# A two-layer decoder trunk on one core: where the second layer's wide Gram copies, Gram products and masks stand in the order of the work

## The chip, the core and the metric

The kernel runs on one core of a Trainium2 chip. Time is what the device needs for one execution, in microseconds (us); the median of the runs counts, and less is better. The engines are named as in the profile: PE (TensorE, matmuls), PEld (PE's weight loads, which overlap its matmuls), DVE (VectorE), ACT (ScalarE), POOL (GpSimd) and SP (SyncE, which here only starts transfers). Each engine carries out its own instructions strictly in the order in which they were put into its queue.

## The reference

Two residual layers over 512 positions of width 2048. Layer 0 is gated differential attention, which the change does not touch. Layer 1 is gated RWKV-7 time mixing with 32 heads of width 64:

```python
def step(S, inp):
    r_t, w_t, k_t, v_t, a_t, b_t = inp
    sa = jnp.einsum('bhvk,bhk->bhv', S, a_t)
    S = S * w_t[:, :, None, :] + sa[..., None] * b_t[:, :, None, :] + v_t[..., None] * k_t[:, :, None, :]
    y = jnp.einsum('bhvk,bhk->bhv', S, r_t)
    return S, y
...
p = h @ w_in                                  # 2048 -> 4*2048 + 2*96
p = p + (token_shift(p) - p) * mu
r, k, v, g, dw, da = jnp.split(p, RW_SPLITS, axis=-1)
...
y = wkv7_scan(rh, heads(decay), kh, vh, -kk, kk * ah)
y = (y - mean) * lax.rsqrt(var + GN_EPS)      # per head, then gain, bias and a bonus term
y = y.reshape(B, T, RW_WIDTH) * jax.nn.silu(g)
return y @ w_out, v_first                     # and x + this
```

All in float32, so each large product is computed as three matmuls on operands that are split into a high and a low part.

## The kernel before, in words

**Split products.** A weight tile `wraw` (eight blocks of 128x128) is loaded by SP, cast by ACT to its high part `wh` (L115), and DVE subtracts to get the low part `wl` (L116), four blocks at a time. One projection of 128 columns is 16 blocks of three matmuls with 512 columns (L129): 48 on PE. `unit_chan` issues them, and after every block a *hook* may run: `behind=[(18, f)]` calls `f` when 18 of the 48 have been issued.

**Rounds.** Layer 1 runs 16 rounds, j = 0 to 15, each for one pair of heads: the projections to keys (`proj(1, j)`), receptances (`proj(0, j)`), values (`proj(2, j)`) and, three rounds later, gates (`proj(3, j - 3)`). The scan of pair j − 1 runs inside round j.

**The chunked scan.** 512 positions are eight chunks of 64. For every pair three things are made first. `gram` (L1136): 32 small matmuls into four PSUM tiles `gp` (tags pb and pc, two buffers each), from which ACT copies the small triangles `LP` (eight copies of 32x128, L1144) and the wide Gram matrices `G` (four copies of 128x512, L1148); in the kernel before the two kinds alternate on ACT as the scheduler chooses. `mask_gram`: four affine selects on POOL (L1174, L1176) that zero parts of `G`. `t_solve`: a triangular solve on DVE, which begins with the transpose `LT` of `LP` (L1208) and goes on in pairs of small steps (L1221, L1224), paced by PE's matmuls, until the transposes to `T` (L1229) and `W` (L1234); then `t_first` (px products, L1255) and `t_second` (L1270) make the inverse `TT` with POOL's and ACT's help.

`scan_pair` then does, for each chunk c, on one PSUM tile `sm`:

- W: one product of G and VS (L1347); ACT copies the result to `rhs` (L1350, two copies)
- X: one product of TT and `rhs` (L1360); ACT copies it into `VS` (L1362, two copies)
- K: one product of BKT and VS (L1367); DVE adds the decayed state and writes the next chunk's `VS` (L1374 for c = 0, L1371 after)

The next W needs that VS. So the scan is a chain PE, ACT, PE, ACT, PE, DVE, and the kernel fills the time between its products with the matmuls of the projections: a `Chain` object counts matmuls (`tick`) and issues the next product after a fixed number, the gaps: (7, 8) in rounds 3 to 14, (5, 6) in round 2, (4, 5) in rounds 1 and 15.

**What sets the order.** A scheduler orders each engine's queue by readiness and priority: scan (`SCAN`) before solve (`SOLVE`) before work marked `AHEAD` (weight splits, the LP copies, the group norm) before the rest, where the G copies are. `issue_after` ties a piece of work behind an instruction in the order. `g.soon` is a list of deferred pieces; `soon(g)` issues all that is in it, and `scan_pair` calls it right behind the copies of `rhs`, inside a scan step:

```python
for h, r_ in HEADS:
    rc = nc.scalar.copy(rhs[r_, :], sm[r_, h * C : h * C + C])
with g.tc.issue_after(rc.ins):
    soon(g)
```

**Neighbours.** `norms` sends sums of squares (`ssl`, L1160) through DRAM with POOL's transfers `nd<-ssl` and `n<-nd` (L1164, L1167); the buffer of `ssl` is shared with `ysq` (L1414), the squares of the group norm of pair j − 2, which is followed on DVE by a sum, a Newton rsqrt (L63 to L70) and a product with `yc` (L1420). `turn_keys` transposes the keys (L1189) to `BKT` (L1190).

Of the kernel before, what the change touches and what calls it, by code (L numbers as in the profile page):

```python
# [23 lines left out]
P = 128  # L24
D = 2048
# [886 lines left out]
def split_act(g, src, pool, tag):  # L912
    nc = g.nc
    hh = pool.tile(list(src.shape), F32R, name="sH" + tag, tag=tag + "H", bufs=1)
    hl = pool.tile(list(src.shape), F32R, name="sL" + tag, tag=tag + "L", bufs=1)
    nc.scalar.copy(hh[:], src)
    nc.vector.tensor_sub(hl[:], src, hh[:].bitcast(F32))
    return hh, hl


def unit_chan(g, parts, cols, step=P, more=None, behind=(), pts=None):

    nc = g.nc
    n = cols // step
    pts = pts or [g.pp.tile([P, 512], F32, name="pp", tag="pp") for _ in range(n)]
    KG = 8 if cols == P else 4
    m = None
    for k0 in range(0, KT, KG):
        wh, wl = split_w(g, parts, KG, cols, k0)
        for k, c in [(k, c) for k in range(KG) for c in range(n)]:  # L930
            s = slice(c * step, (c + 1) * step)
            kk = k0 + k
            if more and c == 0:
                more(kk + 2, m)
            m = mm3(nc, pts[c][:step, :], wh[:, k, s], wl[:, k, s], g.hH[kk][:], g.hL[kk][:],
                    kk == 0, kk == KT - 1, g)
            for at, follow in behind:
                if 3 * kk + 3 == at:
                    follow(m)
    return pts  # L940


@urgent
def shift_mix(g, ps, rows, mu, omu, tag, bufs=2):

    nc, w = g.nc, g.work
    o_ = w.tile([P, T], F32, name="mix" + tag, tag=tag, bufs=bufs)
    nc.scalar.activation(o_[:rows, :], ps[:rows, :], AF.Copy, scale=omu)
    nc.vector.scalar_tensor_tensor(o_[:rows, 1:], ps[:rows, 0 : T - 1], mu, o_[:rows, 1:], ALU.mult, ALU.add)
    return o_  # L950
# [84 lines left out]
def mus(g, i, j):  # L1035
    n = i * 16 + j
    return g.mu[:, n : n + 1], g.omu[:, n : n + 1]


def sum_channels(g, out, ones, x):  # L1040

    h, l = x
    g.nc.tensor.matmul(out, ones, h[:], start=True, stop=False)
    g.nc.tensor.matmul(out, ones, l[:], start=False, stop=True)


def soon(g):
    while g.soon:
        g.soon.pop(0)()
# [76 lines left out]
def gram(g, j, p):  # L1126

    nc, w, BK = g.nc, g.work, p.BK
    p.G = w.tile([P, NC_, 2, 2, C], F32, name="G1", tag="G1", bufs=2)
    halves = []  # L1130
    for c0, tag in ((0, "pb"), (4, "pc")):
        gp = [g.ps.tile([P, 512], F32, name="gp", tag=tag, bufs=2) for _ in range(2)]
        halves.append((c0, gp))
        for i in range(4):
            for h, r_ in ((0, slice(0, C)), (1, slice(C, P))):
                m = nc.tensor.matmul(gp[h][:, i * P : (i + 1) * P], BK[r_, c0 + i, :, :], p.AR[r_, c0 + i, :, :],  # L1136
                                     start=True, stop=True)
    p.LP = w.tile([P, NC_, HALF], F32, name="LP", tag="tmpl", bufs=1)
    with g.tc.high_priority(offset=AHEAD):
        for c0, gp in halves:  # L1140
            for h in range(2):
                for half in range(2):
                    q, o = h * C + half * HALF, half * HALF
                    nc.scalar.copy(p.LP[q : q + HALF, c0 : c0 + 4],  # L1144
                                   gp[h][q : q + HALF].rearrange("p (u x) -> p u x", u=4)[:, :, o : o + HALF])
    for c0, gp in halves:
        for h in range(2):
            nc.scalar.copy(p.G[:, c0 : c0 + 4, :, h, :], gp[h][:].rearrange("p (u x t) -> p u x t", u=4, x=2))  # L1148


def norms(g, j, p, m):
# [18 lines left out]
def mask_gram(g, p, h, m=None):  # L1170

    nc = g.nc
    for r_ in [slice(h * C, h * C + C)]:
        a = nc.gpsimd.affine_select(out=p.G[r_, :, 0, 1 - h, :], in_=p.G[r_, :, 0, 1 - h, :], compare_op=ALU.is_ge,  # L1174
                                fill=0.0, base=-1, pattern=[[0, NC_], [1, C]], channel_multiplier=-1)
        b = nc.gpsimd.affine_select(out=p.G[r_, :, 1], in_=p.G[r_, :, 1], compare_op=ALU.is_ge, fill=0.0, base=0,  # L1176
                                pattern=[[0, NC_], [0, 2], [1, C]], channel_multiplier=-1)
        behind(g, a, m)
        behind(g, b, m)


def turn_keys(g, p, c0):

    nc = g.nc
    if not c0:
        p.BKT = g.work.tile([P, NC_, P], F32, name="BKT", tag="BKT", bufs=2)
    ps = g.ps.tile([P, 512], F32, name="pt", tag="pb", bufs=2)
    for i in range(4):
        nc.tensor.transpose(ps[:, i * P : (i + 1) * P], p.BK[:, c0 + i].rearrange("p s t -> p (s t)"), g.ident[:])  # L1189
    nc.scalar.copy(p.BKT[:, c0 : c0 + 4], ps[:].rearrange("p (c k) -> p c k", c=4))  # L1190


def behind(g, ins, m=None):

    m = m or g.at
    if m:
        g.tc.add_manual_dep(ins.ins, m.ins.name, mybir.DependencyInfo(mybir.DependencyClass.NoSync,
                            mybir.DependencyReason.DATA), reason="pace")
# [80 lines left out]
def stage_v(g, j, p, vps):  # L1279
    nc, w = g.nc, g.work  # L1280
    col = lambda n: g.prm[n][:, j : j + 1]
    ps = g.ps.tile([P, 512], F32, name="pt", tag="pd", bufs=1)
    sum_channels(g, ps[:], g.ones[:], split_act(g, p.rf[:], w, "x"))
    v = shift_mix(g, vps, P, *mus(g, 2, j), "v", 1)
    p.y = w.tile([P, T], F32, name="y", tag="y", bufs=4)
    nc.vector.tensor_mul(p.y[:], ps[:], v[:])
    nc.scalar.activation(p.y[:], p.y[:], AF.Identity, bias=col("hgb"))
    p.v = v


def turn_values(g, p):

    nc, w, v = g.nc, g.work, p.v
    p.VS = w.tile([P, NC_, 2, C], F32, name="VS", tag="VS", bufs=2)
    ps = g.ps.tile([P, 512], F32, name="pt", tag="pd", bufs=1)
    for t in range(NT):
        nc.tensor.transpose(ps[:, t * P : (t + 1) * P], v[:, t * P : (t + 1) * P], g.ident[:])
    pv = ps[:].rearrange("p (t h n) -> p t h n", t=NT, h=2)
    for h in range(2):
        for par in range(2):  # L1300
            nc.scalar.copy(p.VS[(1 - h) * C : (2 - h) * C, par : NC_ : 2, h, :], pv[par * C : par * C + C, :, h, :])
# [130 lines left out]
def layer1(g, aps):  # L1432
    nc, tc = g.nc, g.tc
    with ExitStack() as cx:
# [7 lines left out]
        def proj(i, j, **k):  # L1442
            return unit_chan(g, [(win, i * D + j * P, P)], P, **k)[0]
# [24 lines left out]
        for j in range(D // P):  # L1468
            p = pairs[j]
            if j:  # L1470
                others = [(1, lambda p=p: turn_keys(g, p, 0)), (2, lambda p=p: turn_keys(g, p, 4)),
                          (4, lambda p=p: turn_values(g, p))]
                if j > 1:
                    others.append((5, lambda i=j - 2: finish_y(g, i, pairs[i])))
                full = LAG <= j < D // P - 1
                gaps = (7, 8) if full else (5, 6) if j == 2 else (4, 5)
                chain(g, j - 1, pairs[j - 1], 3 if j > 1 else 22, *gaps, others)
            stage2(g, j, r, p)

            def behind(m, j=j, p=p):  # L1480
                if j > 1:
                    pairs[j - 2].chain.finish(g)
                with tc.issue_after(m.ins):
                    gram(g, j, p)
                if j + 1 == D // P:
                    mask_gram(g, p, 0)
                    mask_gram(g, p, 1)
                p.solve = Solve(g, t_solve(g, j, p))
            stage_v(g, j, p, proj(2, j, behind=[(18, behind)]))
            if j == 0:  # L1490
                turn_keys(g, p, 0)
                turn_keys(g, p, 4)
                turn_values(g, p)
            if j + 1 < D // P:
                begin(j + 1)
            if j >= LAG:
                gated(g, j - LAG, pairs[j - LAG], gate(g, j - LAG, proj(3, j - LAG)))
            if j + 1 < D // P:
                r = receptances(j + 1)
                if j:  # L1500
                    with tc.high_priority(offset=AHEAD):
                        group_norm(g, j - 1, pairs[j - 1])
# [53 lines left out]
        for nm in ("11", "21", "22", "12"):  # L1556
            t, c = PLACES[nm]
# [66 lines left out]
```

## Time and profile before

| | |
|---|---|
| median of 3 runs | 2167.13 us (2166.67 to 2170.02) |
| the profiled execution | 2167.93 us, its span 2166.2 us |
| mean granted clock of PE | 0.998 |
| PE, PEld busy | 98%, 81% of the span |
| DVE, ACT, POOL busy | 71%, 52%, 15% |

The profile is of one execution, 0.80 us above the median. A row of its timeline has the start (us from the span's start), the duration, the engine, the line, the operation with what it writes and reads, the shape, and, in brackets, how long the engine had been idle and who released it. Layer 1's rounds lie between 1030 and 1990 us. A matmul's rows and its weight load's (PEld) are apart; of the load it is read when PE first could not go on.

### The profile page before, as it was taken

The page shows a single profiled execution, that of the slowest core. Times are in us where ns is not written, and L with a number is a line of the kernel's source. Part 1 is how long each engine was busy: PE and PEld are TensorE (multiplying, and loading weights), DVE is VectorE, ACT ScalarE, POOL GpSimd, SP SyncE. Part 2 cuts the span into 40 slices and gives each one's busy share as a digit, 9 for nine tenths or more (in the row PEclk, how much of TensorE's full clock was granted, in tenths as well). Part 3 has the DMA queues.
Part 4 walks back from the last instruction along what each step waited for, and adds up shares of the span by engine and source line. Part 5 has one row for each costly group of instructions (what it writes and reads, how often), then busy time and mean ns, then how long its engine had stood idle before and what let it go on. Part 6 is the DMA issues. An engine that isn't in the chain of part 4 may idle for free.

```text
span 2166.2 us, 34954 instructions
## 1 busy us (share of the span) xinstructions
PE 2132.2 (98%) x12260; PEld 1755.7 (81%) x12260; DVE 1544.3 (71%) x4137; ACT 1124.0 (52%) x2587; POOL 334.1 (15%) x614
## 2 busy tenths in 40 slices
PE   9999999999999999999999999999999999999999
PEld 8888888888888878888777888888888888877887
DVE  5665647465656667467788888888888888887645
ACT  6443444343444455345566656666666666665333
POOL 0000000000000000021132322323333332232001
PEclk9999999999999999999999999999999999999999
DMA  6223232222223365662222232322223223345565
GB/s 196 90 87 98 79 102 85 96 95 86 92 88 98 98 204 189 181 139 80 81 59 55 76 81 79 82 76 76 76 76 86 76 66 81 84 123 185 178 168 121
DMA packets 258624, 225.77 MB, mean 104 GB/s; under 512 B 12336, under 2 KB 220480, under 8 KB 258448
## 3 DMA queue, kind: packets, MB, share of 16 engines
q1 hardware_dynamic: 239504, 188.03, 29.2%
q0 software_dynamic: 10080, 19.50, 4.5%
q10 hardware_dynamic: 8864, 16.01, 2.0%
q8 instruction: 96, 1.57, 0.3%
q14 instruction: 80, 0.66, 0.1%
HBM read 207.50 MB, written 15.99 MB: 103 GB/s over the span
## 4 chain that ended last, share of the span: by engine, by line
PE 89%; DVE 5%; ACT 4%; issue 1%; DMA 1%; POOL 0%; DVEq 0%; ACTq 0%; POOLq 0%
PE pp L129 69%; PE pt L129 5%; ACT G L1148 1%; ACT LP L1144 1%; PE o L129 1%; PE sc L129 1%; PE sm L1360 1%; PE sm L1367 1%; PE sm L1347 1%; PE lora L129 1%; DVE wl L116 1%; PE gp L1136 1%; PE Y L1389 1%; DMA yr<-yd 1%; PE pt L346 1%
## 5 line engine op out<-in xcount | busy, mean ns | idle before, releaser
L116 DVE TENSOR_TENSOR wl<-wraw,wh 128x512 fp32r<-128x512 f32 (+1 forms) x636 | 446.8, 705 | 388.3 <-ACT wh L115 379.3
L115 ACT CAST wh<-wraw 128x512 fp32r<-128x512 f32 (+1 forms) x636 | 393.1, 619 | 524.4 <-PE pp L129 416.9
L129 PE MATMUL pp<-wh,hH 128*128 128x512 f32 x1268 | 500.1, 394 | 0.8 <-DVE prmin_rw_mu_dram L234 0.6
L129 PE MATMUL pp<-wh,hL 128*128 128x512 f32 x1268 | 497.5, 393 | 0.0
L129 PE MATMUL pp<-wl,hH 128*128 128x512 f32 x1268 | 497.0, 392 | 0.0
L129 PE MATMUL pp<-hH,wh 128*128 128x512 f32 x1024 | 418.3, 408 | 0.0
L129 PE MATMUL pp<-hL,wh 128*128 128x512 f32 x1024 | 414.0, 404 | 0.0
L129 PE MATMUL pp<-hH,wl 128*128 128x512 f32 x1024 | 413.9, 404 | 0.0
L129 PEld LDWEIGHTS pp<-wh,hH 128*128 128x128 f32 x1268 | 238.3, 188 | 49.1 <-issue 1.3
L129 PEld LDWEIGHTS pp<-wh,hL 128*128 128x128 f32 x1268 | 238.2, 188 | 48.6
L129 PEld LDWEIGHTS pp<-wl,hH 128*128 128x128 f32 x1268 | 238.3, 188 | 46.8
L129 PEld LDWEIGHTS pp<-hH,wh 128*128 128x128 f32 x1024 | 193.5, 189 | 38.3 <-issue 2.0
L129 PEld LDWEIGHTS pp<-hH,wl 128*128 128x128 f32 x1024 | 193.9, 189 | 33.4
L129 PEld LDWEIGHTS pp<-hL,wh 128*128 128x128 f32 x1024 | 193.8, 189 | 32.3
L1355 POOL COPY SA<-VS 64x64 f32<-64x64 f32 x224 | 78.6, 351 | 470.5 <-DVE VS L1371 411.2
L1221 DVE SCALAR_TENSOR_TENSOR tmpl<-LT,n,Tm 128x60 f32<-128x60 f32 (+24 forms) x496 | 136.3, 275 | 13.8
L500 POOL DMA_DIRECT2D frow<-yd x12 | 8.9, 742 | 803.1 <-DVE rs_t L67 675.7
L1224 DVE TENSOR_TENSOR Tm<-Tm,tmpl 128x60 f32<-128x60 f32 (+24 forms) x496 | 112.0, 226 | 13.0
L1362 ACT COPY VS<-sm 64x64 f32<-64x64 f32 x256 | 52.9, 207 | 61.3 <-PE sm L1360 49.4
L1350 ACT COPY rhs<-sm 64x64 f32<-64x64 f32 x256 | 52.8, 206 | 58.4 <-PE sm L1347 56.3
L1360 PEld LDWEIGHTS sm<-rhs,TT 128*128 128x128 f32 x256 | 46.1, 188 | 29.9 <-ACT rhs L1350 18.4
L1371 DVE SCALAR_TENSOR_TENSOR VS<-sm,gam,Sg 64x64 f32<-64x64 f32 x192 | 54.1, 282 | 20.0 <-PE sm L1367 15.4
(339 smaller groups left out, 3263.9 us busy)
## 6 DMA issues: line engine op xcount, KB each, us to landing
wraw<-in_rw_w_in_dram SPq DMA_DIRECT2D x128, 512.0 KB, 4.0
wraw<-in_da_w_in_dram SPq DMA_DIRECT2D x254, 256.0 KB, 3.0
wraw<-in_da_w_out_dram SPq DMA_DIRECT2D x26, 512.0 KB, 4.3
wraw<-in_rw_w_out_dram SPq DMA_DIRECT2D x26, 512.0 KB, 4.2
yr<-yd SPq DMA_DIRECT2D x28, 256.0 KB, 3.5
frow<-yd POOLq DMA_DIRECT2D x12, 512.0 KB, 6.1
xq<-in_x_dram SPq DMA_DIRECT2D x16, 256.0 KB, 5.4
xd<-xq ACTq DMA_DIRECT2D x16, 256.0 KB, 3.9
```

What stands on the lines that cost most here:

```text
L115: nc.scalar.copy(hi[:], raw[:, k : k + n])
L116: nc.vector.tensor_sub(lo[:], raw[:, k : k + n], hi[:].bitcast(F32))
L129: m = nc.tensor.matmul(out, a, b, start=s, stop=e, skip_group_check=skip)
L346: nc.tensor.transpose(pt[:, c * P : (c + 1) * P], t1s[t][:, c * P : (c + 1) * P], g.ident[:])
L1136: m = nc.tensor.matmul(gp[h][:, i * P : (i + 1) * P], BK[r_, c0 + i, :, :], p.AR[r_, c0 + i, :, :], start=True, stop=True)
L1221: st = nc.vector.scalar_tensor_tensor(tt, LT[:, i : i + 1, i + 1 :].to_broadcast([P, s, n]), n2[:, i : i + 1], Tm[:, 0:s, i : i + 1].to_br ...
L1224: nc.vector.tensor_add(Tm[:, 0:s, i + 1 :], Tm[:, 0:s, i + 1 :], tt)
L1350: rc = nc.scalar.copy(rhs[r_, :], sm[r_, h * C : h * C + C])
L1355: nc.gpsimd.tensor_copy(p.SA[r_, c - 1, :], VS[r_, c, h, :])
L1360: nc.tensor.matmul(sm[:, P : P + C], both(g.TT[j % 2][:, c]), rhs[:], start=True, stop=True)
L1362: nc.scalar.copy(VS[r_, c, h, :], sm[r_, P : P + C])
L1371: g.state = nc.vector.scalar_tensor_tensor(VS[r_, c + 1, h, :], s_, p.gam[r_, c : c + 1], Sg[r_, :], ALU.mult, ALU.add)
```

## The change

Three edits, all in layer 1.

1. In `gram` the four wide G copies become a function `grams` that is put on `g.soon`, so that they are issued right behind the next copies of `rhs`, as part of the scan step. In round 0, where no scan runs, they are issued at once.
2. The hook that calls `gram` stands at 12 matmuls of the values' projection instead of 18 in rounds 1 and 2.
3. In round 15 the masks (`mask_gram`) are issued at 39 matmuls of that projection instead of together with `gram`.

```diff
-    for c0, gp in halves:
-        for h in range(2):
-            nc.scalar.copy(p.G[:, c0 : c0 + 4, :, h, :], gp[h][:].rearrange("p (u x t) -> p u x t", u=4, x=2))
+
+    def grams():
+        for c0, gp in halves:
+            for h in range(2):
+                nc.scalar.copy(p.G[:, c0 : c0 + 4, :, h, :], gp[h][:].rearrange("p (u x t) -> p u x t", u=4, x=2))
+
+    g.soon.append(grams)
+    if not j:
+        soon(g)
...
                 with tc.issue_after(m.ins):
                     gram(g, j, p)
-                if j + 1 == D // P:
-                    mask_gram(g, p, 0)
-                    mask_gram(g, p, 1)
                 p.solve = Solve(g, t_solve(g, j, p))
-            stage_v(g, j, p, proj(2, j, behind=[(18, behind)]))
+            hooks = [(12 if 0 < j < 3 else 18, behind)]
+            if j + 1 == D // P:
+                hooks.append((39, lambda m, p=p: [mask_gram(g, p, h, m) for h in range(2)]))
+            stage_v(g, j, p, proj(2, j, behind=hooks))
```

From `grams` on the lines of the changed kernel are up to six higher: L1148 becomes L1150, L1347 L1353, L1350 L1356, L1360 L1366, L1362 L1368, L1367 L1373, L1371 L1377, L1374 L1380.

ACT's queue in round 8, from the cast ahead of the group norm's squares to the copy of the keys' transposes (G_15643 is this pair's G). Before:

```order
L916 CAST sHx<-mixr 128x512
L1414 ACTIVATE ysq<-yc 128x512
L1144 COPY LP<-gp 32x128 x4
L1148 COPY G_15643<-gp 128x8x64 x2
L1144 COPY LP<-gp 32x128 x4
L1148 COPY G_15643<-gp 128x8x64 x2
L115 CAST wh<-wraw 128x512
L1350 COPY rhs<-sm 64x64 x2
L1362 COPY VS<-sm 64x64 x2
L115 CAST wh<-wraw 128x512
L1190 COPY BKT<-pt 128x512
```

And in the changed kernel:

```order
L916 CAST sHx<-mixr 128x512
L1420 ACTIVATE ysq<-yc 128x512
L1144 COPY LP<-gp 32x128 x8
L115 CAST wh<-wraw 128x512
L1356 COPY rhs<-sm 64x64 x2
L1150 COPY G_15643<-gp 128x8x64 x4
L1368 COPY VS<-sm 64x64 x2
L115 CAST wh<-wraw 128x512
L1196 COPY BKT<-pt 128x512
```

The four G copies have moved from between and behind the LP copies to behind the rhs copies, where they stand ahead of the VS copies; the order is the same in rounds 3 to 14.

DVE's queue in round 2, around the group norm and the first chunk's state (L1374, now L1380). Before:

```order
L116 TENSOR_TENSOR wl<-wraw,wh 128x512
L1374 TENSOR_SCALAR VS<-sm,gam 64x64 x2
L917 TENSOR_TENSOR sLx<-mixr,sHx 128x512
L1416 TENSOR_REDUCE var<-ysq 128x8
L1417 TENSOR_SCALAR var<-var 128x8
```

And in the changed kernel, where sLx and the sum (L1422) stand in the same order and twelve rows further on comes:

```order
L67 TENSOR_TENSOR rs_t<-rs_i 128x8
L68 SCALAR_TENSOR_TENSOR rs_t<-rs_t,var 128x8
L1380 TENSOR_SCALAR VS<-sm,gam 64x64 x2
L70 SCALAR_TENSOR_TENSOR rsg<-rs_t,rs_i 128x8
L1426 TENSOR_TENSOR yc<-yc,rsg 128x512
L1214 STREAM_TRANSPOSE LT<-LP 128x32x32
```

The state's instruction has moved from ahead of the group norm's sum to ahead of the last step of its rsqrt.

## The prediction

> **What bounds the kernel now.** I read the page's busy shares first, then the list of waits of TensorE (PE) in the second layer, then the timeline of one round.
>
> ```profile
> PE 2132.2 (98%) x12260; PEld 1755.7 (81%) x12260; DVE 1544.3 (71%) x4137; ACT 1124.0 (52%) x2587; POOL 334.1 (15%) x614
> PE sm L1360 <- ACT rhs L1350: 11.5, 15, 3.1
> ```
>
> PE is busy 98% of the span, so a change that leaves PE's work as it is can only bring back the gaps. The second row is the largest of them: fifteen waits of X = TT·rhs (L1360) for the copies of its right-hand side on ScalarE (ACT), 11.5 us in all, the longest 3.1. That is the wait at which the change aims. Twelve of the fifteen stand in rounds 3 to 14, one in each and alike; the first and the last of them:
>
> ```profile
> 1202.26 0.43 PE L1360 MATMUL sm<-rhs,TT 128*128 128x64 f32 x2 [0.55 <-ACT rhs L1350]
> 1863.87 0.43 PE L1360 MATMUL sm<-rhs,TT 128*128 128x64 f32 x2 [0.55 <-ACT rhs L1350]
> ```
>
> Eleven rounds lie between them, 661.61 / 11 = 60.15 us each. Round 8 on ACT and PE, in order of time (start, duration; rows without PE's stream of projections except the three that date it; the first two rows are the same step one chunk earlier, where nothing waits):
>
> ```profile
> 1494.09 0.39 PE L129 MATMUL pp<-hH,wh 128*128 128x512 f32 x1
> 1494.46 0.48 PE L129 MATMUL pp<-hL,wh 128*128 128x512 f32 x1
> ...
> 1497.91 1.06 ACT L1144 COPY LP<-gp 32x128 f32<-32x128 f32 x4 [1.09 <-PE gp L1136]
> ...
> 1500.43 0.38 PE L1347 MATMUL sm<-VS,G 128*128 128x128 f32 x2
> 1501.03 1.08 ACT L1148 COPY G<-gp 128x512 f32<-128x512 f32 x2
> 1501.99 0.63 ACT L115 CAST wh<-wraw 128x512 fp32r<-128x512 f32 x1
> 1502.04 0.40 PE L129 MATMUL pp<-hL,wh 128*128 128x512 f32 x1
> 1502.51 0.43 ACT L1350 COPY rhs<-sm 64x64 f32<-64x64 f32 x2
> 1502.99 0.43 PE L1360 MATMUL sm<-rhs,TT 128*128 128x64 f32 x2 [0.55 <-ACT rhs L1350]
> 1503.23 0.47 PE L129 MATMUL pp<-hH,wl 128*128 128x512 f32 x1
> 1503.52 0.44 ACT L1362 COPY VS<-sm 64x64 f32<-64x64 f32 x2 [0.58 <-PE sm L1360]
> 1504.70 0.42 PEld L1367 LDWEIGHTS sm<-VS,BKT 128*128 128x128 f32 x2
> ```
>
> W (L1347) is through at 1500.81, but ACT works off the Gram copies and a weight cast and comes to rhs only at 1502.51. Without a wait an X between two projections makes the second start 0.37 after the first (1494.09 to 1494.46); here it is 1503.23 − 1502.04 = 1.19. The stall is 0.82 us a round.
>
> VectorE (DVE) in the same stretch, with PE's two later W loads (the window row gives busy us of PE, PEld, DVE, ACT, POOL, then the clock):
>
> ```profile
> 1495.80:1506.80 11.00, 10.45 (x75) 8.53 (x74) 10.21 (x29) 7.55 (x21) 1.14 (x4) 1.00 0.19 50
> 1501.40 2.16 DVE L1208 STREAM_TRANSPOSE LT<-LP 128x1024 f32<-128x1024 f32 x1
> 1506.20 0.60 DVE L1371 SCALAR_TENSOR_TENSOR VS<-sm,gam,Sg 64x64 f32<-64x64 f32 x2
> 1507.20 0.42 PEld L1347 LDWEIGHTS sm<-VS,G 128*128 128x128 f32 x2
> 1507.57 0.48 PE L129 MATMUL pp<-hH,wl 128*128 128x512 f32 x1
> 1512.85 0.59 DVE L1371 SCALAR_TENSOR_TENSOR VS<-sm,gam,Sg 64x64 f32<-64x64 f32 x2
> 1513.85 0.42 PEld L1347 LDWEIGHTS sm<-VS,G 128*128 128x128 f32 x2
> ...
> 1929.76 0.60 DVE L1371 SCALAR_TENSOR_TENSOR VS<-sm,gam,Sg 64x64 f32<-64x64 f32 x2
> 1930.47 0.30 PEld L1347 LDWEIGHTS sm<-VS,G 128*128 128x128 f32 x2 [1.46 <-issue]
> ```
>
> DVE is busy 10.21 of 11.0 us, 29 instructions almost end to end. It is full, and it writes the next W's operand (VS, L1371) at 1506.80, only 0.40 before that W loads. This is what the change runs into. The last pair, of round 15, shows a W that does wait: the load follows the end of VS (1930.36) by 0.11.
>
> **Rounds 3 to 14, part by part.** The new order on ACT is eight LP copies, cast, rhs, four G copies, VS copies. LP's eight take 2 × 1.06 from 1497.91, to 1500.03; the cast 0.63, to 1500.66; rhs can start when W is through, about 1500.9, and ends near 1501.3 instead of 1502.94. X then needs no wait: it and all behind it come 0.82 earlier. The G copies, two pairs of 1.08, 2.15 us, run to 1503.45 and the VS copies to 1503.9; K (L1367) would like to load at 1504.70 − 0.82 = 1503.88 (seven projections behind X's load, 1.71 us, 0.24 each with what lies between). K loses 0.1 at most, which the next term swallows. The count on ACT, PE and DVE is unchanged; only the order moves.
>
> What is late next is W at 1507.20. Ahead of VS on DVE stand the same instructions as before (the new weight split now ahead of LT instead of behind it), DVE has no idle time to give, so VS still ends at 1506.80. W loads at 1506.80 + 0.11 = 1506.91. A load that waited is followed by the next projection after 0.24 (1502.99 to 1503.23), one that didn't after 0.37 (1507.20 to 1507.57), so that projection starts at 1507.15, against 1507.57: 0.42 is left of 0.82. The next VS ends at 1513.44, 0.41 ahead of its load, so the same lead passes there. Twelve rounds at 0.41: 4.9 us. The bounds are 0 (the whole wait moves to W or K) and 12 × 0.82 = 9.8 (VS comes earlier too). I take 4.9 since both rows that set it stand in this stretch.
>
> **Round 1.**
>
> ```profile
> 1090.87 2.07 DVE L1208 STREAM_TRANSPOSE LT<-LP 128x1024 f32<-128x1024 f32 x1 [2.79 <-ACT LP L1144]
> 1092.39 0.41 PE L1360 MATMUL sm<-rhs,TT 128*128 128x64 f32 x2 [1.51 <-ACT rhs L1350]
> 1095.00 0.42 PEld L1347 LDWEIGHTS sm<-VS,G 128*128 128x128 f32 x2
> 1123.64 0.46 PE L1347 MATMUL sm<-VS,G 128*128 128x128 f32 x2 [1.32 <-DVE VS L1371]
> ```
>
> and the two halves of a solve step on DVE, all of them grouped (busy us, mean ns of one):
>
> ```profile
> L1221 DVE SCALAR_TENSOR_TENSOR tmpl<-LT,n,Tm 128x60 f32<-128x60 f32 (+24 forms) x496 | 136.3, 275 | 13.8
> L1224 DVE TENSOR_TENSOR Tm<-Tm,tmpl 128x60 f32<-128x60 f32 (+24 forms) x496 | 112.0, 226 | 13.0
> ```
>
> The wait of 1.51 goes: the Gram products come earlier, and rhs stands ahead of G. W would then load at 1095.00 − 1.51 = 1093.5. But VS of chunk 0 now stands behind LT, its norms and three solve steps. LP is done sooner by the G pair that lay between its halves, 1.08, and by some of six projections of 0.24; I take 1.4 together, so LT starts at 1089.5 and ends at 1091.6. Three steps of 0.28 + 0.23, some 0.6 for the norms and the gaps, VS itself 0.6 and 0.11 to the load bring W to about 1094.4. So some 0.5 of the 1.51 is gained. Of the wait at 1123.64 the solve's head start takes perhaps 0.3. I take 0.8; bounds 0 and 2.8 (both waits gone).
>
> **Round 2.**
>
> ```profile
> 1142.66 0.42 PEld L1347 LDWEIGHTS sm<-VS,G 128*128 128x128 f32 x2
> 1142.85 0.63 ACT L1414 ACTIVATE ysq<-yc 128x512 f32<-128x512 f32 x1 [2.72 <-DMA nd<-ssl]
> 1146.50 0.17 DVE L70 SCALAR_TENSOR_TENSOR rsg<-rs_t,rs_i 128x8 f32<-128x8 f32 x1
> 1147.58 0.43 PE L1360 MATMUL sm<-rhs,TT 128*128 128x64 f32 x2 [3.15 <-ACT rhs L1350]
> 1148.50:1151.90 3.40, 3.40 (x13) 2.91 (x12) 2.54 (x6) 1.05 (x4) 1.05 (x3) 0.50 0.00 0
> ...
> 1187.90 0.69 PE L1255 MATMUL px<-T,G 32*32 32x32 f32 x32 [0.74 <-DVE T L1229]
> ```
>
> Here a 3.15 us wait, and after it 3.40 us at a granted clock of 0.50 (1.7 us lost), look like the largest single prize. I don't believe that it is paid out. In the new DVE order VS of chunk 0 stands just ahead of the last step of the rsqrt (L70, 1146.50), behind a chain that starts with ysq, and ysq waits for the DMA nd<-ssl until 1142.85, whoever is queued behind. VS would end at 1147.1 and W load at 1147.2, where it loaded at 1142.66 without a wait. X follows W's load by 1.62 (1142.66 to 1147.58, less 3.15 and the 0.15 of its late start), so it comes at 1148.7, about 1.1 later than now. Round 1's quicker solve may bring that DMA forward, I allow 0.4; the px products come eight matmuls sooner and wait longer for T, I allow 0.4 more loss on the 0.74. The clock's 1.7 is lost as before. Total −1.1; bounds −2.5 (no lead, and px waiting 1.4 more, which is 8 × 0.24 less part of what W lost) and +4.8 (all of wait and clock).
>
> [...]
>
> **Round 15.**
>
> ```profile
> 1923.24 0.49 PE L1367 MATMUL sm<-VS,BKT 128*128 128x128 f32 x2 [1.40 <-ACT VS L1362]
> 1925.63 0.43 ACT L1350 COPY rhs<-sm 64x64 f32<-64x64 f32 x2 [0.83 <-PE sm L1347]
> 1927.24 0.42 PEld L1367 LDWEIGHTS sm<-VS,BKT 128*128 128x128 f32 x2
> ```
>
> K's wait of 1.40 goes, since the VS copies no longer stand behind G. The G copies go behind the following rhs instead, and there VS stands behind them and a BKT copy: rhs ends at 1926.06, and 2.15 + 0.6 + 0.44 later, at 1929.25, VS is there, where K loaded at 1927.24 and now, four transposes later, would at about 1927.7. It waits 1.5. The W at 1930.47 waited 1.46 for VS behind solve steps; a K that late hides most of that, I count 0.8 back. The selects move to a place some 70 projections, 17 us, before their reader, so nobody waits for them; DVE steps beside them may take longer, which I put at nothing. Sum 1.4 − 1.5 + 0.8 = 0.7; bounds −1.0 and 2.5.
>
> **Sum.** 4.9 + 0.8 − 1.1 + 0.7 = 5.3. The profiled execution took 2167.93, 0.80 above the median of 2167.13, so it would become 2162.6, and the median 2161.8.
>
> **The rivals.** *Full gain.* If VS on DVE is not bound (the scheduler's order makes DVE's stretch start earlier as well), rounds 3 to 14 give 9.8, the sum 10.2, time 2156.9. For it: LT's input is ready 1 us sooner. Against: 10.21 of 11.0 busy. 0.15.
>
> *The wait moves whole.* K and then W take up all of the 0.82: twelve rounds give 0, the rest 0.4, time 2166.7. For it: K has no slack (1503.9 against 1503.88), and W only 0.40 less 0.11. 0.18.
>
> *Slower: rhs comes no sooner, and four G copies stand ahead of VS.* The cast ahead of rhs needs a free weight buffer; in the trace it ran at 1501.99 behind a busy ACT, which leaves open from when it could. If it still runs there, rhs ends at 1502.94, G at 1505.1, VS at 1505.5, and K loads 0.88 later than now: 12 × 0.88 = 10.6 lost, less 0.4, time 2177.3. It turns at a rhs that ends at 1502.06 (1504.70 − 2.15 − 0.44 − 0.05). Against: it started the moment ACT came free (no idle time stands in its row), so nothing but ACT is seen to hold it. 0.11.
>
> **How the numbers follow.** The forecast has 0.56, with a range of its own from 2159 to 2165 (half of either bound). A measurement of this kernel can tell about 0.2%, 4.3 us, from no change: the lines are 2162.8 and 2171.5. Of the forecast's 0.56 I put 0.12 above 2162.8. Faster: 0.44 + 0.15 = 0.59. Same: 0.12 + 0.16 of the second rival = 0.28. Slower: 0.11 + 0.02 = 0.13. The range that leaves out the slower rival and the ends of the others: 2155.5 to 2167.2.
>
> **What would show it.** In rounds 3 to 14 X without a wait, and in its place W's load with a wait of some 0.1 to 0.3 released by VS (L1371, now L1377), rounds 59.74 us apart; in round 2 a wait of W (now L1353) of 3 to 4.5 us behind a late ysq, and half clock again; in round 15 K waiting once, one step later. It is wrong if the rounds come 0.8 closer (DVE had room), or if the L1356 copies still end behind PE's X, or if round 2's W doesn't wait.

## The result and the profile after

Over 20 runs each the changed kernel takes 2162.88 us (2160.22 to 2166.95) against 2167.03 us (2164.94 to 2170.06): ratio 0.9979, 95% interval 0.9972 to 0.9986. That is 4.15 us, just under the 0.2% that the prediction counted as no change, and 1.1 us above the forecast. The sum came out; its terms did not.

The list of PE's waits in the second layer of the changed kernel (what waited, for whom, us in total, times, longest):

```profile
PE sm L1353 <- DVE VS L1377: 9.3, 16, 2.2
PE pt L1303 <- DVE Tm L1230: 3.0, 1, 3.0
PE sm L1353 <- DVE VS L1380: 2.4, 2, 1.2
PE px L1261 <- DVE T L1235: 1.9, 3, 0.9
PE sm L1366 <- ACT rhs L1356: 0.3, 1, 0.3
```

X's wait for rhs on ACT fell from 11.5 us to 0.3. In its place W (L1353) waits for DVE, 9.3 + 2.4 = 11.7 us: the bottleneck of the scan changed its engine.

Since the projections' matmuls are the same in both kernels, the time at which one and the same of them starts can be compared at the ends of the rounds. The change, in us of the two profiled executions:

| stretch | after minus before | forecast |
|---|---|---|
| up to round 0 (nothing changed there) | +1.9 | 0 |
| round 0 (nothing changed there): half clock before, none after | −1.6 | 0 |
| round 1 | −1.0 | −0.8 |
| round 2 | −2.7 | +1.1 |
| rounds 3 to 14 | −2.4 | −4.9 |
| round 15 | +1.8 | −0.7 |
| span | −4.0 | −5.3 |

The first two rows are not the change: single executions differ so. What the change touched adds up to −4.3, near the 4.15 of the medians. Single rows move by up to 0.3 with the matmul that is taken as the end of a round. Round 2's −2.7 holds 1.7 us of half clock that only the execution before has (0.50 over 1148.5 to 1151.9), and round 15's +1.8 holds 1.7 us that only the one after has.

**Rounds 3 to 14.** W in the first and the last of them, and DVE ahead of it in round 8 (the row of the window has busy us of PE, PEld, DVE, ACT and POOL, then PE's clock):

```profile
1203.05 0.46 PE L1353 MATMUL sm<-VS,G 128*128 128x128 f32 x2 [0.39 <-DVE VS L1377]
1862.17 0.46 PE L1353 MATMUL sm<-VS,G 128*128 128x128 f32 x2 [0.38 <-DVE VS L1377]
```

```profile
1491.30:1502.50 11.20, 10.98 (x77) 8.94 (x75) 10.37 (x29) 7.80 (x22) 1.13 (x4) 1.00 0.24 68
```

```profile
1496.30 0.69 DVE L1426 TENSOR_TENSOR yc<-yc,rsg 128x512 f32<-128x512 f32 x1
1496.91 0.69 DVE L116 TENSOR_TENSOR wl<-wraw,wh 128x512 fp32r<-128x512 f32 x1
1497.52 2.23 DVE L1214 STREAM_TRANSPOSE LT<-LP 128x1024 f32<-128x1024 f32 x1
1499.65 0.13 DVE L1222 TENSOR_SCALAR n<-n 128x32 f32<-128x32 f32 x1
1499.81 0.35 DVE L1223 RECIPROCAL n<-n 128x32 f32<-128x32 f32 x1
1500.28 0.25 DVE L1227 SCALAR_TENSOR_TENSOR tmpl<-LT,n,Tm 128x31 f32<-128x31 f32 x1
...
1501.19 0.69 DVE L116 TENSOR_TENSOR wl<-wraw,wh 128x512 fp32r<-128x512 f32 x1
1501.91 0.60 DVE L1377 SCALAR_TENSOR_TENSOR VS<-sm,gam,Sg 64x64 f32<-64x64 f32 x2
...
1502.65 0.46 PE L1353 MATMUL sm<-VS,G 128*128 128x128 f32 x2 [0.37 <-DVE VS L1377]
```

On ACT, in the same round, rhs stands ahead of the four G copies, and X has no wait:

```profile
1495.69 0.62 ACT L115 CAST wh<-wraw 128x512 fp32r<-128x512 f32 x1
1496.37 0.42 ACT L1356 COPY rhs<-sm 64x64 f32<-64x64 f32 x2
1496.82 2.06 ACT L1150 COPY G<-gp 128x512 f32<-128x512 f32 x4
1498.73 0.46 ACT L1368 COPY VS<-sm 64x64 f32<-64x64 f32 x2
```

The rounds now come (1862.17 − 1203.05) / 11 = 59.92 us apart, 0.23 closer. DVE is as full as before, 10.37 of 11.2 us. VS is written at 1502.51, and W follows it. That is the mechanism that was forecast; the next section shows why less came of it.

**Round 2.** ACT's and DVE's rows around the group norm, and W:

```profile
1139.12 0.62 ACT L1420 ACTIVATE ysq<-yc 128x512 f32<-128x512 f32 x1
1142.76 0.59 DVE L1380 TENSOR_SCALAR VS<-sm,gam 64x64 f32<-64x64 f32 x2
1143.49 0.46 PE L1353 MATMUL sm<-VS,G 128*128 128x128 f32 x2 [1.19 <-DVE VS L1380]
1147.00:1152.00 5.00, 4.95 (x26) 3.93 (x27) 4.59 (x17) 2.43 (x7) 1.47 (x3) 1.00 0.18 41
```

POOL's transfers of ssl, before and after:

```profile
1136.94 1.18 POOL L1164 DMA_DIRECT2D nd<-ssl  x2 [0.21 <-issue]
1143.30 0.58 POOL L1167 DMA_DIRECT2D n<-nd  x1 [5.18 <-DMA nd<-ssl]
```

```profile
1134.77 1.18 POOL L1170 DMA_DIRECT2D nd<-ssl  x2 [0.92 <-ACT ssl L1166]
1137.83 0.58 POOL L1173 DMA_DIRECT2D n<-nd  x1 [1.88 <-DMA nd<-ssl]
```

They start 2.2 us earlier (0.65 of it because all of PE is earlier there), and the second of them lands 1.88 us after its issue instead of 5.18. The two traces show what goes with that. In the kernel before, SP issues a weight load of 512 KB 0.26 us ahead of the second transfer (1137.31 against 1137.56), and the transfer lands 0.16 us after that load (1142.74 after 1142.58). In the change the load is issued 0.84 us behind it (1136.23 against 1135.39). The waits of POOL for the transfer follow the place of the Gram products: 5.31 us with them at 18 (e1), 1.88 to 1.91 at 12 (e2, e3 and e4). No run moved the load alone, so that its place is the cause is not shown. So ysq, which has no idle time ahead of it in its row, does not wait for them. VS does stand behind the rsqrt, as the order said, but W waits only 1.19 us for it, and PE keeps its full clock.

**Round 15.** POOL's selects, DVE's solve steps beside them, the state, and W:

```profile
1924.59 0.28 DVE L1227 SCALAR_TENSOR_TENSOR tmpl<-LT,n,Tm 128x52 f32<-128x52 f32 x1
1924.90 1.22 DVE L1230 TENSOR_TENSOR Tm<-Tm,tmpl 128x52 f32<-128x52 f32 x1
1924.91 1.15 POOL L1182 TENSOR_SCALAR_AFFINE_SELECT G<-G 64x1024 f32<-64x1024 f32 x1
1926.16 0.67 DVE L1227 SCALAR_TENSOR_TENSOR tmpl<-LT,n,Tm 128x50 f32<-128x50 f32 x1
1926.72 1.17 POOL L1182 TENSOR_SCALAR_AFFINE_SELECT G<-G 64x1024 f32<-64x1024 f32 x1
1926.86 1.09 DVE L1230 TENSOR_TENSOR Tm<-Tm,tmpl 128x50 f32<-128x50 f32 x1
1929.25 0.59 DVE L1377 SCALAR_TENSOR_TENSOR VS<-sm,gam,Sg 64x64 f32<-64x64 f32 x2
...
1929.98 0.72 PE L1353 MATMUL sm<-VS,G 128*128 128x128 f32 x2 [2.20 <-DVE VS L1377]
1930.00:1936.00 6.00, 6.00 (x26) 5.13 (x27) 4.23 (x14) 3.57 (x10) 1.78 (x5) 0.72 0.29 83
```

A step's half that takes 0.2 to 0.3 us alone takes 1.22 and 1.09 beside a select, and ends with it (1924.91 + 1.15 = 1926.06, the step 1926.12). VS comes at 1929.84, W waits 2.20 us, and after it six us have a mean clock of 0.72, so 0.28 × 6 = 1.7 us more are lost in this execution.

### The profile page after: what moved, and what is told of

Same layout as the page of the kernel before. It is cut to its first block, busy times and chain, and to the rows that moved or that the text cites. A ratio compares the mean times of both kernels' runs of the same rounds, so it can differ in the third digit from the quotient of the medians.

```text
span 2162.2 us, 34954 instructions
## 1 busy us (share of the span) xinstructions
PE 2130.9 (99%) x12260; PEld 1752.8 (81%) x12260; DVE 1547.3 (72%) x4137; ACT 1125.5 (52%) x2587; POOL 335.2 (16%) x614
## 4 chain that ended last, share of the span: by engine, by line
PE 85%; DVE 11%; issue 2%; ACT 1%; DMA 1%; POOL 0%; DVEq 0%; ACTq 0%; POOLq 0%
PE pp L129 66%; PE pt L129 5%; DVE wl L116 2%; DVE LT L1214 1%; PE sm L1353 1%; PE o L129 1%; PE sc L129 1%; PE lora L129 1%; PE sm L1373 1%; PE sm L1366 1%; DMA yr<-yd 1%; DVE tmpl L1227 1%; PE Y L1395 1%; DVE Tm L1230 1%; PE pt L346 1%
## 5 line engine op out<-in xcount | busy, mean ns | idle before, releaser
L1356 ACT COPY rhs<-sm 64x64 f32<-64x64 f32 x256 | 52.7, 206 | 61.8 <-PE sm L1353 58.9
L1368 ACT COPY VS<-sm 64x64 f32<-64x64 f32 x256 | 53.0, 207 | 59.1 <-PE sm L1366 48.0
L1353 PEld LDWEIGHTS sm<-VS,G 128*128 128x128 f32 x256 | 45.0, 189 | 29.8 <-PE pp L129 12.9
L1377 DVE SCALAR_TENSOR_TENSOR VS<-sm,gam,Sg 64x64 f32<-64x64 f32 x192 | 54.1, 282 | 18.7 <-PE sm L1373 14.2
```

The lines of the kernel that those rows point to most:

```text
L1353: nc.tensor.matmul(sm[:, 0:P], both(p.G[:, c, 0]), both(VS[:, c]), start=True, stop=True)
L1368: nc.scalar.copy(VS[r_, c, h, :], sm[r_, P : P + C])
L1377: g.state = nc.vector.scalar_tensor_tensor(VS[r_, c + 1, h, :], s_, p.gam[r_, c : c + 1], Sg[r_, :], ALU.mult, ALU.add)
```

## The experiments

All are compared with the kernel before, on the same chip: 2167.11 us beside e1 to e4, 2167.65 us on another chip beside e5 to e8. "e3" and the like are the labels.

**e1: the second edit undone.**

```diff
-            hooks = [(12 if 0 < j < 3 else 18, behind)]
+            hooks = [(18, behind)]
```

> The change with its second edit undone: the Gram products stand at 18 matmuls again in rounds 1 and 2, the deferral of the G copies and the late masks stay. Theory A: the gain of rounds 1 and 2 (about 1.1 and 2.6 us in the profiles) needs the earlier Gram products: T and so the transfers of ssl come earlier, ysq does not wait for them and the state's W in round 2 waits only 1.2 us, too little for the half clock. Without it ysq waits again, W waits some 4 us, PE drops to half clock: 2.5 to 4 us slower than the change, 2165 to 2167. Rival B: the gain comes from rhs standing ahead of G alone: within 1 us of the change, 2162 to 2164. Rounds 3 to 14 stay 59.92 us under both.

Measured: 2162.77 us, ratio 0.9978 (0.9969 to 0.9987), the same as the change: rival B. But theory A's mechanism is there. In its round 2 the transfers of ssl land late and ysq waits:

```profile
1141.21 0.63 ACT L1420 ACTIVATE ysq<-yc 128x512 f32<-128x512 f32 x1 [2.88 <-DMA nd<-ssl]
1138.34 0.59 DVE L1380 TENSOR_SCALAR VS<-sm,gam 64x64 f32<-64x64 f32 x2
```

Only, with the Gram products at 18, VS stands in its old place ahead of the rsqrt (1138.34) and W waits for nothing; what waits is X, 1.82 us instead of 3.15, with the four G copies no longer ahead of rhs, and PE keeps its clock (1.00 over 1147 to 1152 us). By matched matmuls rounds 1 and 2 gain 1.8 and 1.9 us, where the change gains 1.0 and 2.7; rounds 3 to 14 come 59.99 us apart. The two orders cost nearly the same. So the gain of rounds 1 and 2 comes from rhs ahead of G as well as from the earlier products, whichever is there; in round 2, 1.7 us of it are in both the half clock that follows the 3.15 us wait of the kernel before.

**e2: the second edit alone, on the kernel before.**

```diff
-            stage_v(g, j, p, proj(2, j, behind=[(18, behind)]))
+            stage_v(g, j, p, proj(2, j, behind=[(12 if 0 < j < 3 else 18, behind)]))
```

> The kernel before with the second edit alone: Gram products at 12 matmuls in rounds 1 and 2, G copies and masks where they were. Theory A: LP and G are copied 1.4 us sooner, so the rhs copies of rounds 1 and 2 wait less, and the transfers of ssl go out earlier: 2 to 4 us faster than before, 2163 to 2165, with rounds 3 to 14 at 60.15 us. Rival B (order, not time, is what counted): 2166 to 2167.5.

Measured: 2163.70 us, ratio 0.9986 (0.9977 to 0.9994). Rounds 1 and 2 gain 0.4 and 3.2 us by matched matmuls (1.7 of it the half clock again), rounds 3 to 14 nothing. Theory A. So six matmuls of head start in two rounds give most of what the whole change gives. With e1: either edit gains in rounds 1 and 2, together they gain it once.

**e3: the change, and the solve's steps later in rounds 3 to 14.**

```diff
         nc.vector.reciprocal(n2[:], n2[:])
+    full = LAG <= j < D // P - 1
+    if full:
+        yield 12
     for i in range(HALF - 1):
...
-        yield 3 + i % 2
+        yield 3 if full else 3 + i % 2
```

> The change, and in rounds 3 to 14 the solve's steps begin 12 matmuls later (and go on at 3 matmuls a step instead of 3 and 4 in turn), so that one half step instead of two whole steps stands ahead of the state's VS on VectorE. Theory A: VectorE, which is full in that stretch, is what W waits for since the change (0.54 us a round); some 0.7 us less ahead of VS takes that wait away, the rounds come at 59.3 to 59.5 us, and the time falls by 5 to 7.5 us to 2155.5 to 2158. Rival B: K or the VS copies on ScalarE behind the four G copies hold the round: rounds stay at 59.9 us and the time within 1 us of 2162.9. If the solve ends too late for the px products, a wait of px shows instead.

Measured: 2156.67 us, ratio 0.9954 (0.9942 to 0.9967). Theory A. W has no wait left in rounds 3 to 14, and PE's Gram products of the first and the last of these rounds are (1846.43 − 1193.74) / 11 = 59.34 us apart:

```profile
1193.74 2.06 PE L1136 MATMUL gp<-AR,BK 64*128 64x128 f32 x32
1846.43 2.06 PE L1136 MATMUL gp<-AR,BK 64*128 64x128 f32 x32
```

60.15 − 59.34 = 0.81 is the whole stall of X that the prediction had measured (0.82). DVE was what took 0.6 of it back.

**e7: the same late solve on the kernel before**, without anything of the change (the diff is that of e3).

> The kernel before, with the solve's steps 12 matmuls later in rounds 3 to 14 as in e3 and nothing of the change. Theory A: there X's wait for rhs on ScalarE holds the round and VectorE is hidden: rounds stay at 60.15 us, 2166 to 2168. Rival B: the late solve is a gain of its own: 2159 to 2162.

Measured: 2167.12 us, ratio 0.9997 (0.9988 to 1.0006). Theory A: its waits in rounds 3 to 14, with the row of the kernel before ahead of it:

```profile
PE sm L1360 <- ACT rhs L1350: 6.6, 12, 0.6
```

```profile
PE sm L1363 <- ACT rhs L1353: 6.6, 12, 0.6
```

Its rounds stay 60.14 us apart. So the two limits stand one behind the other: ACT first, DVE 0.2 us later. Taking the first away alone gave 0.2 us a round, the second alone 0, both 0.81.

**e5: the change, with DVE's order ahead of VS as it was before.**

```diff
     NQ = HALF // NG
-    yield 9
+    full = LAG <= j < D // P - 1
+    yield 8 if full else 9
...
         nc.vector.reciprocal(n2[:], n2[:])
+    if full:
+        yield 9
...
-        yield 3 + i % 2
+        yield 3 if full else 3 + i % 2
```

> The change, with the solve in rounds 3 to 14 paced so that VectorE's queue ahead of the state's VS is again that of the kernel before: LT, norms, weight split, reciprocal, two steps, weight split, VS (the change has the split ahead of LT). Theory A: the 0.2 us a round between the forecast (0.41) and the change (0.215) is what that order costs, since the split no longer fills the pause between the norms and the reciprocal: W's wait falls from 0.54 to 0.35 or so, rounds 59.7 us, 2 to 2.5 us faster than the change, 2160 to 2161. Rival B: LT itself or another thing is slower beside the G copies: rounds stay at 59.9.

Measured: 2160.53 us, ratio 0.9967 (0.9955 to 0.998). The time is theory A's; the rounds come 59.82 us apart, between the two. DVE's rows from LT to the first step, in its round 8:

```profile
1494.52 2.24 DVE L1215 STREAM_TRANSPOSE LT<-LP 128x1024 f32<-128x1024 f32 x1
1496.63 0.16 DVE L1223 TENSOR_SCALAR n<-n 128x32 f32<-128x32 f32 x1
1496.68 0.71 DVE L116 TENSOR_TENSOR wl<-wraw,wh 128x512 fp32r<-128x512 f32 x1
1497.28 0.37 DVE L1224 RECIPROCAL n<-n 128x32 f32<-128x32 f32 x1
1497.76 0.25 DVE L1230 SCALAR_TENSOR_TENSOR tmpl<-LT,n,Tm 128x31 f32<-128x31 f32 x1
```

The instructions ahead of VS are those of the change, but from the start of yc to that of VS it takes a median of 5.48 us over the twelve rounds, where the change takes 5.61 and the kernel before 5.40. Ahead of LT a weight split puts LT off by 0.61 us (1496.91 to 1497.52 in the change). Between the norms and the reciprocal that reads them it puts the reciprocal off by 0.49 (it starts 0.65 us after the norms here, 0.16 in the change). That is 0.12 less. W's waits over the twelve rounds fall accordingly, the change's row first:

```profile
PE sm L1353 <- DVE VS L1377: 4.6, 12, 0.4
```

```profile
PE sm L1356 <- DVE VS L1380: 3.1, 12, 0.3
```

That explains 0.13 of the 0.21 by which VS comes later in the change. The other 0.08 lies in LT, from its start to the next instruction's: 2.03 us before, 2.13 in the change, 2.11 here. It now runs beside more of ACT's G copies; whether they are the cause was not tried by itself.

**e6: the wide copies behind the VS copies instead of behind those of rhs.**

```diff
-    g.soon.append(grams)
-    if not j:
-        soon(g)
+    g.wide.append(grams)
+    if not j:
+        wide(g)
...
-            nc.scalar.copy(VS[r_, c, h, :], sm[r_, P : P + C])
+            vc = nc.scalar.copy(VS[r_, c, h, :], sm[r_, P : P + C])
+        with g.tc.issue_after(vc.ins):
+            wide(g)
```

> The change, with the wide G copies issued behind the VS copies of the scan instead of behind those of rhs, so that ScalarE has rhs, VS, then G. Theory A: ScalarE is no longer what rounds 3 to 14 wait for, so only what this does to VectorE's order counts: the rounds stay within 0.25 us of 59.92 and the time within 3 us of 2162.9. Rival B: K waits for VS behind the four G copies and hands the wait on to W: rounds 0.4 to 0.6 us shorter, 2155.5 to 2158.

Measured: 2160.37 us, ratio 0.9967 (0.9955 to 0.998). The rounds are 59.80 us apart and W waits 3.2 us over the twelve of them: within theory A, with the state's VS 0.12 earlier on DVE, where the new order put a third step in the place of the second split. Four G copies (2.1 us) more or less ahead of VS on ACT are not what the rounds wait for.

**e4: round 15's masks one projection later.** They cannot go back to the Gram products by themselves, since the copies that they mask now come later; so their place was moved.

```diff
-                hooks.append((39, lambda m, p=p: [mask_gram(g, p, h, m) for h in range(2)]))
+                masks = [(39, lambda m, p=p: [mask_gram(g, p, h, m) for h in range(2)])]
...
-                gated(g, j - LAG, pairs[j - LAG], gate(g, j - LAG, proj(3, j - LAG)))
+                gated(g, j - LAG, pairs[j - LAG], gate(g, j - LAG, proj(3, j - LAG, behind=masks if j + 1 == D // P else ())))
```

> The change with round 15's masks issued at 39 matmuls of the projection that follows (the gates) instead of at 39 of the values' projection. Theory A: beside the selects VectorE's solve steps take 0.7 to 1.2 us instead of 0.2 to 0.3, and where the change puts them they hold the state's VS: W waits 2.2 us and PE then drops to half clock (some 1.6 us). Moved away from that W, the wait goes and the time falls by 2 to 4 us to 2159 to 2161. Rival B: the solve runs all along there, so the selects meet it and another W wherever they stand: 2162 to 2163.5, with the wait at a later W.

Measured: 2161.82 us, ratio 0.9978 (0.9969 to 0.9987): between the two, and not to be told from the change. The wait of 2.2 us is gone, but a later W, at which the selects now stand, waits:

```profile
1941.74 0.46 PE L1353 MATMUL sm<-VS,G 128*128 128x128 f32 x2 [1.17 <-DVE VS L1377]
```

PE keeps its full clock behind it (its projections still come 0.23 us apart, 1942.27 to 1942.50), and by matched matmuls round 15 costs 0.15 us less than before instead of 1.8 more.

**e8: e3, and the masks behind the end of the scan.**

```diff
-            if j + 1 == D // P:
-                hooks.append((39, lambda m, p=p: [mask_gram(g, p, h, m) for h in range(2)]))
...
-        gated(g, j - 2, pairs[j - 2], gate(g, j - 2, proj(3, j - 2)))
+        masks = [(24, lambda m: [mask_gram(g, p, h, m) for h in range(2)])]
+        gated(g, j - 2, pairs[j - 2], gate(g, j - 2, proj(3, j - 2, behind=masks)))
```

> e3 (the change with the late solve in rounds 3 to 14), and round 15's masks at 24 matmuls of the gate projection that follows the loop, where the scan of the pair before is over. Theory A: the selects then meet no state's VS, the wait of 2.2 us and the half clock behind it go: 1.5 to 3.5 us faster than e3, 2153 to 2155.5. Rival B: the selects slow the solve, T comes later and px waits instead: within 1 us of e3, 2156 to 2157.5.

Measured: 2152.25 us (2151.40 to 2153.44), ratio 0.9930 (0.9917 to 0.9944), the fastest of all: 15.4 us under its kernel before, where the change is 4.15 under its own. Theory A: W's waits for L1380, 4.7 us with 2.2 the longest in e3, fall to

```profile
PE sm L1356 <- DVE VS L1380: 2.8, 4, 1.1
```

in the whole layer, and the selects meet no state that PE waits for; round 15 is 1.4 us shorter than before. The gain over e3 is 4.4 us by the two medians, and 5.0 with each set against its own kernel before, on its own chip. The profile shows 3.4 of it in round 15 (the wait and the clock behind it). Where the rest lies is not shown; of e3's five executions two have a mean clock of 0.996, e8's all have 0.999.

## Why the prediction was right, and where it was not

The range held the time, and the likeliest case was the right one in its main mechanism. Step by step:

- **rhs ahead of G takes X's wait away in rounds 3 to 14: right.** The 6.6 us of these rounds became 0 (11.5 to 0.3 in the whole layer). K and the copies on ACT lost nothing (e6). The slower rival, that the weight cast ahead of rhs still ran late, fell: it ran as soon as LP was done, and rhs with W.
- **What is late next is W, since VS on DVE does not move: right, and shown** by e3 and e7 together. The rival of the full gain was wrong for the change, and became true in e3.
- **The size, 0.41 a round: mis-sized; the rounds came 0.23 closer, and W waits 0.38 where 0.1 to 0.3 was forecast.** The failing step is "Ahead of VS on DVE stand the same instructions as before (the new weight split now ahead of LT instead of behind it) ... so VS still ends at 1506.80". The same instructions in another order took 0.21 longer. I had summed busy time and not looked at what stands between an instruction and the one that reads it; e5 gives 0.13 for that, and 0.08 lies in a longer LT, whose cause stays open.
- **Round 1: right in size** (1.0 against 0.8), with the wait of W as described.
- **Round 2: wrong, by 3.8 us and in sign.** The failing step is that the transfers of ssl hold ysq until 1142.85 in the changed kernel too ("Round 1's quicker solve may bring that DMA forward, I allow 0.4"). They went out 2.2 us earlier, the second landed after 1.88 us instead of 5.18, and both had landed by 1137.8, more than a microsecond before ysq was due at 1139.1. I had taken the end time of a transfer as fixed in a kernel in which both its start and the weight load beside it move. The half clock that I had counted as lost did not come either. (A slip besides: 1147.2 + 1.62 is 1148.8, not 1148.7.)
- **Round 15: wrong, by 2.5 us and in sign.** The failing step is "DVE steps beside them may take longer, which I put at nothing". The load of the first K waits 0.41 and that of the second not at all, so the price of 1.5 that I had set on the second K did not come; the selects' did, on the W behind. That leaves 0.4 us lost in e1, where no half clock followed (1.00 over 1930 to 1936 us), and 1.8 in the change, where it did. The trace before had such rows, and I didn't price them; these are from round 1:

```profile
1117.87 1.16 POOL L1176 TENSOR_SCALAR_AFFINE_SELECT G<-G 64x1024 f32<-64x1024 f32 x1
1118.01 1.09 DVE L1224 TENSOR_TENSOR Tm<-Tm,tmpl 128x66 f32<-128x66 f32 x1
```

- **The clock.** The sum had half clock again behind W's new wait of 3 to 4.5 us; the wait was 1.19 us and PE kept its clock (1.00 over 1147 to 1152 us). No run shows that term: it was my estimate from one stretch of the kernel before (0.50 behind the 3.15 us wait). The length of a wait does not decide alone, either. The 3.0 us wait in round 0 (L1297 before, L1303 in the change) was followed by half clock before and in e3 (0.76 and 0.57 over 1054 to 1061 us) and not in the change and e8 (1.00); over the same stretch five of the ten profiles have 0.57 to 0.76 and five 1.00. Round 15's wait of 2.2 us was followed by 0.72 over six us in the change, e3 and e5; e1 and e6, with the masks at the same place, have 1.00 there. At the end of layer 0 a 1.7 us wait (L846) went with 0.79 over 979 to 987 us in the kernel before and 0.85 in the change; the waits of 1.0 to 1.5 us in rounds 1 and 2 of these two were followed by none. In the clock records of their traces half clock comes in stretches of 3.41 us, except at the very end (2.56 and 2.10), and within one execution they start whole multiples of 3.41 us apart (75.10 and 92.16 us, 22 and 27 of them, in the one before; 945.49 us, 277, in the one after). What sets these starts is not shown.

So 5.3 was near 4.15 because two wrong signs and one double size cancelled: −2.5 too much in rounds 3 to 14, −3.8 too little in round 2, +2.5 overlooked in round 15. That the sum came out is luck, and the clock has a part in it: the 1.7 us in round 2 and the 1.7 in round 15 cancel too, and such a stretch comes in some executions only. What the experiments confirm is the mechanism in rounds 3 to 14, not the sum.

Edit by edit: the deferral gives 2.4 us in rounds 3 to 14; either the deferral or the earlier Gram products give the gain in rounds 1 and 2; the masks where the change puts them go with a loss of 0.4 us in round 15, or 1.8 with the half clock, and with a place behind the scan the round gains 1.4.

## What to carry to other kernels

When a wait of the main engine has two causes one close behind the other, removing one shows little (here 0.23 of 0.81 us a round, or nothing): look for the margin of the next releaser (here 0.40 us of VS ahead of W), and move both. Where an engine is full, the order of its instructions can be a cost by itself (0.13 us of DVE's time ahead of VS, e5): put independent work between an instruction and the one that reads it. And before work is moved to a "free" engine or time, look for whose instructions run beside it (a solve step of 1.22 us beside a select), not only for who waits for it.

## What the runs showed of the hardware

Of the solve's half steps on DVE that start beside one of POOL's affine selects, 21 in the trace before and 24 in the one after, every one ends 0.02 to 0.08 us behind that select; with no select beside them none takes more than 0.35 us. Beside the wide selects of round 15 (1.15 and 1.17 us) that made 1.22 and 1.09 us of steps whose mean is 0.23 (L1224 before). What the two engines share there is not shown. And whether half clock follows PE's 3.0 us wait in round 0 differs from execution to execution (0.76 over 1054 to 1061 us before, 1.00 in the change); a stretch of 3.41 us at 0.50 costs some 1.7. This goes with the spread between executions of one kernel: of the 20 of the change, the six with a mean clock of 0.999 took 2161.24 us on average, the thirteen with 0.998 2163.17, and the one with 0.996 2166.95.
